# Reciprocal square roots of 35 row norms: a guess from ScalarE's Sqrt and one Newton step in place of an integer guess and three Newton steps

## The chip, the cores and the metric

The kernel is one program on one core of a Trainium2 chip. It runs one inference step of a small two-layer decoder trunk. The metric is device time in microseconds (us); the number compared is the median over runs. The profile comes from one profiled execution, whose own time stands beside its span below. The engines are named as in the profile: PE is the matrix engine, PEld its weight loads, DVE the vector engine, ACT the scalar engine, POOL the general engine, SP the engine that issues most of the DMAs ("SPq" in its rows). Each engine works through its instructions in order.

## The reference

The trunk has 1024 prompt rows and 64 sample rows of 1024 columns, and two layers. The first has an S5 mixer, the second attention over one shared K/V; each has a convolutional feed-forward block behind it. Around every block stands the same row norm. In the reference, cut to what matters here:

```python
def rmsnorm(x, g):
    xf = x.astype(jnp.float32)
    y = xf * lax.rsqrt(jnp.mean(xf * xf, axis=-1, keepdims=True) + NORM_EPS)
    return (y * g.astype(jnp.float32)).astype(x.dtype)
...
def trunk(x, ssm_h0, conv_buf0, past_k, past_v, p):
    for i in range(DEPTH):
        if i < N_A_LAYERS:
            ...
            x = x + rmsnorm(a_out, p['a_post_g'][i])
        else:
            ...
                kv_in = rmsnorm(x, p['kv_norm_g'])
                k_new = (kv_in @ p['w_k']).reshape(bsz, seq_len, N_HEADS, 2 * HEAD_DIM)
            ...
            x = x + rmsnorm(o @ p['w_o'][j], p['b_post_g'][j])
        f_out, buf = conv_ffn(rmsnorm(x, p['f_pre_g'][i]), conv_buf0[i], p['w_up'][i], p['conv_w'][i],
                              p['conv_b'][i], p['w_down'][i])
        x = x + rmsnorm(f_out, p['f_post_g'][i])
```

What matters is how `rsqrt` of one number per row is computed in the norms behind the output projection (`o @ p['w_o']`) and behind the two down projections (`f_out`), and in the norms of the next block that follow them at once.

## The kernel before

The rows lie in nine token tiles, eight of 128 rows and one of 64 (the samples). The stages follow one another: the S5 mixer and its GLU, the first feed-forward block (`ffn_up(0)`, `ffn_down(0)`), K/V and query projections (`kv_proj`), attention, the output projection (`o_proj`), the second feed-forward block (`ffn_up(1)`, `ffn_down(1)`). PE multiplies in a three-product form, each operand split into a high and a low part (`mm3`, L809 to L811, or L1417); `split_evac` makes such a pair, a CAST on ACT (L144) and a subtraction on DVE (L145).

A finished tile `y` of a projection passes through the "tail":

- `tail_a` closes the block: the sum of squares of the row (`square_sum`, a Square on ACT with an accumulator, L824), the product with the gain (DVE, L851), the reciprocal root `r` (`rstd_from`), then `y * r` plus the residual row in one instruction (DVE, L854). SP stores the result (L855); after the first down projection that is `x2d<-acc`, after the output projection `x3d<-acc`, after the second down projection the program's output.
- `tail_n` is the norm of the next block on that result: again `square_sum`, `rstd_from`, then the product with `r`, on ACT without a gain (L862) or on DVE with one (L864). After the second down projection there is none.
- `tail_b` (or `Combos.pair`) transposes the normed tile on PE (L870) and splits it into the operands `xT_hi` and `xT_lo` of the next projection.

`rstd_from` works on a column of 128 numbers. `rv` is -0.5 times the mean square plus epsilon (L120; L122 where a part of the sum was taken earlier). `rr` begins as an integer guess on the bits of `rv` (L123), and three Newton steps of two instructions follow (L130 writes `rs`, L134 writes `rr`). Each of these eight DVE instructions depends on the one before. With `aside` the Newton steps run on POOL instead.

`Tail` delays the steps: `tail_n` of a tile is issued right behind its `tail_a`, `tail_b` some tiles later. The instructions are not issued in program order: the program is built with a scheduler that simulates a timeline and sets each engine's order by it, so that a change of a few instructions moves others around them.

In `ffn_down`, the operand tiles of the next step are loaded by SP from the scratch tensor `gd` (`gr<-gd`, L1342 or L1355), cast by ACT and multiplied (L1417); partial sums are added to the `acc` tile of their token tile on DVE (L1424 in the last step of the first down projection, L1428 elsewhere). These loads, the residual rows `xr` (L847, L1383) and the stores of finished tiles share SP's queue, in order.

In `o_proj` the second half of the columns is done last, for the tiles in `LATE`; each is copied from PSUM by ACT (L2025), closed by `tail_a` and normed by `tail_n` with a gain (L864), while `ffn_up(1)` already prepares its weights: sums of weight tiles on DVE (L1109 to L1112) and their split into `whi` (ACT) and `wlo` (DVE).

Of the kernel before, what the change touches and what calls it, by code (L numbers as in the profile page):

```python
# [13 lines left out]
I32 = mybir.dt.int32  # L14
AF = mybir.ActivationFunctionType
ALU = mybir.AluOpType
# [5 lines left out]
D = 1024  # L22
# [23 lines left out]
RSQ_MAGIC = float(0x5F3759DF - (1 << 22) - (1 << 30))  # L46
# [27 lines left out]
def trunk_kernel(ctx, tc, I, O):  # L74
    nc = tc.nc
    V = nc.vector
    A = nc.scalar
# [4 lines left out]
    def nm(s):  # L82
        uid[0] += 1
        return f"{s}_{uid[0]}"
# [23 lines left out]
    def flat(t, n=512):  # L108
        return t[:, 0:n]

    def rstd_from(pool, ss, n, parts, tag, n_mean=D, bufs=None, pre=None, aside=False):


        kw = {"bufs": bufs} if bufs else {}
        v = pool.tile([P, n], F32, tag=tag + "v", name=nm("rv"), **kw)
        s = pool.tile([P, n], F32, tag=tag + "s", name=nm("rs"), **kw)
        r = pool.tile([P, n], F32, tag=tag + "r", name=nm("rr"), **kw)
        p = slice(0, parts)
        if pre is None:
            V.tensor_scalar(v[p], ss, -0.5 / n_mean, -0.5 * EPS, op0=ALU.mult, op1=ALU.add)  # L120
        else:
            V.scalar_tensor_tensor(v[p], ss, -0.5 / n_mean, pre, op0=ALU.mult, op1=ALU.add)  # L122
        V.tensor_scalar(r[p].bitcast(I32), v[p].bitcast(I32), -0.5, RSQ_MAGIC, op0=ALU.mult, op1=ALU.add)  # L123
        for _ in range(3):
            if aside:
                GP.tensor_scalar(s[p], r[p], r[p], v[p], op0=ALU.mult, op1=ALU.mult)
                GP.tensor_scalar(r[p], s[p], 1.5, r[p], op0=ALU.add, op1=ALU.mult)
                continue
            if n == 1:
                V.scalar_tensor_tensor(s[p], r[p], r[p], v[p], op0=ALU.mult, op1=ALU.mult)  # L130
            else:
                V.tensor_tensor(s[p], r[p], r[p], ALU.mult)
                V.tensor_tensor(s[p], s[p], v[p], ALU.mult)
            V.scalar_tensor_tensor(r[p], s[p], 1.5, r[p], op0=ALU.add, op1=ALU.mult)  # L134
        return r
# [616 lines left out]
    pools = {}  # L752
# [45 lines left out]
    def slot(tag, shape=None, dtype=F32):  # L798

        al = {"gx": "acc", "post": "acc", "junk": "gr"}  # L800
        shp, bufs = {"acc": ([P, 2 + SEQ + NB * 10], NACC), "gx": ([P, 4, 2 * P], NACC), "gr": ([P, 512], NGR),
                     "xr": ([P, D], 2), "junk": ([P, D], NGR), "post": ([P, D], NACC),
                     "cvo": ([P, 4, 18], 2), "cpar": ([P, 2 * NF, 20], 1), "ss": ([P, 1], 4)}[tag]
        tag = al.get(tag, tag)
        return pools["ph"].tile(shape or shp, dtype, tag=tag, name=nm(tag), bufs=bufs)
# [10 lines left out]
    def row_bcast(src):  # L816
        t = slot("post")
        nc.sync.dma_start(t, src.partition_broadcast(P))
        return t

    def square_sum(y, n):
        junk = slot("junk", dtype=BF16)
        ss = slot("ss")
        A.activation(junk[0:n, 0 : y.shape[1]], y, AF.Square, accum_out=ss[0:n])  # L824
        return ss[0:n]

    sums = {}
# [13 lines left out]
    def tail_a(y, tt, post, xsrc, xdst, last=False, rest=slice(0, D), aside=False, xr=None):  # L841


        t0, n = tokens(tt)
        if xr is None:
            xr = slot("xr")
            nc.sync.dma_start(xr[0:n], xsrc(tt))  # L847
        halves = (slice(512, D), slice(0, 512)) if last else (slice(0, D),)
        ss = square_sum(y[:, rest], n)
        for hs in halves if last else (rest,):  # L850
            V.tensor_tensor(y[:, hs], y[:, hs], post[0:n, hs], ALU.mult)  # L851
        r = rstd_from(pools["ph"], ss, 1, n, "n1", bufs=4, pre=sums.pop(tt, None), aside=aside)
        for hs in halves:
            V.scalar_tensor_tensor(y[:, hs], y[:, hs], r[0:n], xr[0:n, hs], op0=ALU.mult, op1=ALU.add)  # L854
            nc.sync.dma_start(xdst(tt)[:, hs], y[:, hs])  # L855

    def tail_n(y, tt, aside, gain=None):

        n = tokens(tt)[1]
        r = rstd_from(pools["ph"], square_sum(y, n), 1, n, "n1", bufs=4, aside=aside)  # L860
        if gain is None:
            A.mul(y, y, r[0:n])  # L862
        else:
            V.scalar_tensor_tensor(y, y, r[0:n], gain[0:n], op0=ALU.mult, op1=ALU.mult)  # L864
# [55 lines left out]
    class Tail:  # L920
# [2 lines left out]

        def __init__(self):
            self.n, self.q, self.combos, self.gain, self.lag = [], [], None, None, 2

        def add(self, y, tt, *a, aside=False, **kw):
            tail_a(y, tt, *a, aside=aside, **kw)
# [20 lines left out]
    tail = Tail()  # L949
# [422 lines left out]

    def ffn_down(dn, i, xsrc, xdst, norm):
        acc, res = {}, {}
        post = [None]
        nch = len(dn.plan)

# [619 lines left out]
    def o_proj():  # L1997

        ws = half_units(I["w_o"][0], 1)
        post = row_bcast(I["b_post_g"][0])  # L2000
        tail.gain, tail.lag = row_bcast(I["f_pre_g"][1]), 1
        conv_params(1)
        xsx = sample_pair()

        for half, tts in ((1, ORDER_O), (0, LATE)):
# [4 lines left out]
            for tt in tts:  # L2010
                if tt == 0 and half:
                    tail.combos = Combos()
                t0, n = tokens(tt)
                end = half == 0 or tt in EARLY
                if end:
                    y = slot("acc")[0:n, 0:D]
# [87 lines left out]
```

## Time and profile before

| | us |
|---|---|
| median of 3 runs | 2680.4 |
| lowest and highest run | 2679.09, 2680.55 |
| the profiled execution's own time | 2684.83 |
| its span | 2682.9 |
| DVE busy in the span | 1963.5 |
| ACT busy in the span | 1270.9 |
| DVE busy in all L130 (x156), L134 (x204), L123 (x88) | 30.3, 30.8, 13.0 |

A row of the profile's timeline gives the start in us from the span's start, the duration, the engine, the line, the operation, what it writes and reads, and in brackets the idle time before it and what ended that. A row of the windows gives for each engine its busy time in that stretch and the number of instructions, then the granted PE clock, the DMA share and GB/s. A row by line ends with the total and mean duration and the engine's idle time before such instructions. A row of the waits names the waiting instruction, what it waited for, the total, the times and the longest. A row of the chain gives start, length and piece. The durations of neighbouring rows overlap, as an engine starts an instruction before the one ahead of it has ended; how long one holds the engine is read from start to start.

### The profile page before, as it was taken

What the parts mean: (1) busy time and instruction counts of PE and PEld (TensorE: products, weight loads), DVE (VectorE), ACT (ScalarE), POOL (GpSimd) and SP (SyncE); (2) the same over time, 40 slices, a digit from 0 to 9 for tenths busy, and PEclk for the clock granted to TensorE, in tenths of its full rate; (3) what the DMA queues carried; (4) which work ended last, traced back from release to release, by engine and by line L of the source; (5) the groups of instructions that cost most, each with busy time, mean ns of one, the idle gap of its engine ahead of it and who ended that gap; (6) DMA issues with size and microseconds to landing.
All of it is one profiled execution on the core that took longest, in us unless ns stands there. A gap on an engine that the chain in (4) does not pass through costs nothing.

```text
span 2682.9 us, 39622 instructions
## 1 busy us (share of the span) xinstructions
PE 2500.6 (93%) x14234; PEld 2203.5 (82%) x14234; DVE 1963.5 (73%) x3683; ACT 1270.9 (47%) x2559; POOL 657.3 (24%) x1062
## 2 busy tenths in 40 slices
PE   3778998999999989999999899989799999998997
PEld 2777887999999967778777788877699999996775
DVE  7994358777777789984232688875877777778999
ACT  6763334444444454354322677764544444444432
POOL 3220030111111175501201222113011111137661
PEclk9999998999999999999999899999899999999998
DMA  5443233222222233444646433335322222233334
GB/s 145 99 98 88 85 124 124 65 83 74 74 74 74 89 116 92 127 145 166 204 157 211 104 79 95 97 105 171 115 69 79 74 74 74 74 104 107 94 102 145
DMA packets 265688, 286.77 MB, mean 107 GB/s; under 512 B 42268, under 2 KB 212564, under 8 KB 265492
## 3 DMA queue, kind: packets, MB, share of 16 engines
q1 hardware_dynamic: 261892, 273.55, 33.0%
q0 software_dynamic: 3088, 9.77, 1.7%
q8 instruction: 113, 1.85, 0.3%
q10 hardware_dynamic: 512, 0.92, 0.1%
q14 instruction: 83, 0.68, 0.1%
HBM read 193.58 MB, written 70.93 MB: 99 GB/s over the span
## 4 chain that ended last, share of the span: by engine, by line
PE 58%; DVE 13%; DMA 4%; issue 3%; ACT 3%; POOL 2%; SPq 0%; DVEq 0%; POOLq 0%; ACTq 0%
PE mm L809 17%; PE mm L810 17%; PE mm L811 17%; DVE acc L1428 2%; DMA gr<-gd 1%; DVE xT_lo L145 1%; DVE S L1898 1%; PE mm L1417 1%; ACT S L1902 1%; DVE wst L145 1%; DVE xT_hi L145 1%; DVE acc L854 1%; PE mm L1436 1%; PE tr L870 1%; PE mm L1926 1%
## 5 line engine op out<-in xcount | busy, mean ns | idle before, releaser
L809 PE MATMUL mm<-xT_hi,whi 128*128 128x384 f32 (+1 forms) x1408 | 457.0, 325 | 2.0 <-ACT acc L1146 1.8
L810 PE MATMUL mm<-xT_lo,whi 128*128 128x384 f32 (+1 forms) x1408 | 456.3, 324 | 1.6 <-DVE xT_lo L145 1.6
L811 PE MATMUL mm<-xT_hi,wlo 128*128 128x384 f32 (+1 forms) x1408 | 454.2, 324 | 0.0
L809 PEld LDWEIGHTS mm<-xT_hi,whi 128*128 128x128 f32 x1408 | 265.4, 189 | 3.8 <-ACT acc L1146 2.4
L810 PEld LDWEIGHTS mm<-xT_lo,whi 128*128 128x128 f32 x1408 | 265.7, 189 | 2.4 <-DVE xT_lo L145 2.3
L811 PEld LDWEIGHTS mm<-xT_hi,wlo 128*128 128x128 f32 x1408 | 265.4, 189 | 0.8
L1195 POOL COPY cvo<-acc 128x2 f32<-128x2 f32 x88 | 53.3, 606 | 818.5 <-ACT acc L1178 818.5
L809 PE MATMUL mm<-whi,xT_hi 128*128 128x512 f32 x608 | 243.9, 404 | 4.9 <-ACT whi L792 4.7
L1192 DVE SCALAR_TENSOR_TENSOR acc<-acc,cpar,acc 128x1104 f32<-128x1104 f32 x176 | 240.0, 1385 | 4.7 <-ACT acc L1190 4.6
L810 PE MATMUL mm<-wlo,xT_hi 128*128 128x512 f32 x608 | 241.9, 398 | 0.1
L811 PE MATMUL mm<-whi,xT_lo 128*128 128x512 f32 x608 | 241.7, 399 | 0.0
L144 ACT CAST whi<-raw 128x1024 fp32r<-128x1024 f32 x88 | 92.5, 1051 | 253.5 <-PE mm L811 245.2
L1428 DVE TENSOR_TENSOR acc<-mm,acc 128x512 f32<-128x512 f32 x279 | 184.7, 680 | 9.8 <-PE mm L811 9.3
L145 DVE TENSOR_TENSOR wlo<-raw,whi 128x1024 fp32r<-128x1024 f32 x88 | 107.7, 1224 | 107.0 <-PE mm L810 91.6
L809 PE MATMUL mm<-acc,whi 128*128 128x384 f32 x528 | 179.1, 339 | 0.0
L811 PE MATMUL mm<-acc,wlo 128*128 128x384 f32 x528 | 178.7, 339 | 0.0
L810 PE MATMUL mm<-acc,whi 128*128 128x384 f32 x528 | 178.3, 338 | 0.0
L809 PEld LDWEIGHTS mm<-whi,xT_hi 128*128 128x128 f32 x608 | 115.6, 191 | 36.2 <-ACT whi L792 5.6
L810 PEld LDWEIGHTS mm<-wlo,xT_hi 128*128 128x128 f32 x608 | 114.7, 189 | 27.8 <-DVE wlo L793 0.8
L811 PEld LDWEIGHTS mm<-whi,xT_lo 128*128 128x128 f32 x608 | 114.4, 188 | 27.6 <-issue 0.8
L1190 ACT ACTIVATE acc<-acc,cpar 128x1104 f32<-128x1104 f32 x88 | 114.1, 1311 | 18.1 <-DVE acc L1161 11.9
L145 DVE TENSOR_TENSOR wlo<-xr,whi 128x1024 fp32r<-128x1024 f32 x88 | 107.6, 1223 | 16.7 <-ACT whi L144 8.6
(572 smaller groups left out, 6255.9 us busy)
## 6 DMA issues: line engine op xcount, KB each, us to landing
raw<-in_w_up_dram SPq DMA_DIRECT2D x88, 512.0 KB
gd<-acc SPq DMA_DIRECT2D x44, 552.0 KB
raw<-in_w_down_dram SPq DMA_DIRECT2D x44, 512.0 KB
gr<-gd SPq DMA_DIRECT2D x80, 256.0 KB
raw<-in_glu_w_dram SPq DMA_DIRECT2D x40, 256.0 KB
acc<-in_cache_k_dram SPq DMA_DIRECT2D x16, 512.0 KB
acc<-in_cache_v_dram SPq DMA_DIRECT2D x16, 512.0 KB
xj<-in_x_prompt_dram SPq DMA_DIRECT2D x8, 512.0 KB
```

Of the source, the lines that this page charges most:

```text
L144: A.copy(hi_ap, ps_ap)
L145: V.tensor_tensor(lo_ap, ps_ap, hi_ap.bitcast(F32), ALU.subtract)
L809: PE.matmul(out, lh, rh, start=start, stop=False, **kw)
L810: PE.matmul(out, lh, rl, start=False, stop=False, **kw)
L811: PE.matmul(out, ll, rh, start=False, stop=stop, **kw)
L854: V.scalar_tensor_tensor(y[:, hs], y[:, hs], r[0:n], xr[0:n, hs], op0=ALU.mult, op1=ALU.add)
L870: PE.transpose(ps[:, c * n : (c + 1) * n], y[:, c * P : (c + 1) * P], ident[0:n, 0:n])
L1190: A.activation(hc, hb[:, 2 : 2 + TG], AF.Identity, bias=cp[:, ft, 3:4], scale=cp[:, ft, 2:3])
L1192: V.scalar_tensor_tensor(hc, hb[:, tap : tap + TG], cp[:, ft, tap : tap + 1], hc, op0=ALU.mult, op1=ALU.add)
L1195: GP.tensor_copy(co[:, 0:2], hb[:, SEQ : SEQ + 2])
L1417: PE.matmul(pa[h], lt, wt[:, h * 512 : (h + 1) * 512], start=st and j == 0, stop=sp and j == len(seq) - 1)
L1428: V.tensor_tensor(a, ps, a, ALU.add)
```

## The change

`rstd_from` gets an argument `root`. Where it is set and `aside` is not, the integer guess is replaced by a Sqrt on ACT of -2 times `rv` and a RECIPROCAL of it on DVE, and one Newton step follows in place of three. `Tail` gets a field `root`, false at first; `o_proj` and `ffn_down` set it, and `tail_a` and `tail_n` pass it on. `Tail.root` is not reset, so it holds from the first down projection on. Norms on POOL (`aside`) and the norms of the S5 stage and of attention remain as they were.

```diff
-    def rstd_from(pool, ss, n, parts, tag, n_mean=D, bufs=None, pre=None, aside=False):
+    def rstd_from(pool, ss, n, parts, tag, n_mean=D, bufs=None, pre=None, aside=False, root=False):
...
-        V.tensor_scalar(r[p].bitcast(I32), v[p].bitcast(I32), -0.5, RSQ_MAGIC, op0=ALU.mult, op1=ALU.add)
-        for _ in range(3):
+        root = root and not aside
+        if root:
+            A.activation(s[p], v[p], AF.Sqrt, scale=-2.0)
+            V.reciprocal(r[p], s[p])
+        else:
+            V.tensor_scalar(r[p].bitcast(I32), v[p].bitcast(I32), -0.5, RSQ_MAGIC, op0=ALU.mult, op1=ALU.add)
+        for _ in range(1 if root else 3):
...
-        r = rstd_from(pools["ph"], ss, 1, n, "n1", bufs=4, pre=sums.pop(tt, None), aside=aside)
+        r = rstd_from(pools["ph"], ss, 1, n, "n1", bufs=4, pre=sums.pop(tt, None), aside=aside, root=tail.root)
...
-        r = rstd_from(pools["ph"], square_sum(y, n), 1, n, "n1", bufs=4, aside=aside)
+        r = rstd_from(pools["ph"], square_sum(y, n), 1, n, "n1", bufs=4, aside=aside, root=tail.root)
...
             self.n, self.q, self.combos, self.gain, self.lag = [], [], None, None, 2
+            self.root = False
...
     def ffn_down(dn, i, xsrc, xdst, norm):
         acc, res = {}, {}
+        tail.root = True
...
-        tail.gain, tail.lag = row_bcast(I["f_pre_g"][1]), 1
+        tail.gain, tail.lag, tail.root = row_bcast(I["f_pre_g"][1]), 1, True
```

The lines behind the change carry other numbers: L851 becomes L857, L854 L860, L862 L868, L864 L870, L145 L151, L144 L150, L1424 L1433, L1428 L1437, L2025 L2034; the new Sqrt is L126, the RECIPROCAL L127, the Newton step L136 and L140. In the built program DVE has 140 instructions fewer, ACT has 35 Sqrts and three table loads more, and PE, POOL and SP have as many as before. Where the scheduler now puts things is shown at three places. In the names the first number is that of the tile and is the same in both programs.

First, DVE's queue near the end of the first down projection, before the change. acc_1323 and acc_1314 are two neighbouring output tiles, acc_1327 is the next one; L854 of acc_1314 lets SP store that tile and then issue the next load of gr:

```order
L851 TENSOR_TENSOR acc_1323_8851<-acc_1323_8851,acc_1539_10511 128x1024
...
L1424 TENSOR_TENSOR acc_1327_8878<-mm_1620_10876,acc_1327_8878 128x512
L1424 TENSOR_TENSOR acc_1327_8878<-mm_1621_10877,acc_1327_8878 128x512
...
L130 SCALAR_TENSOR_TENSOR rs_1592_10749<-rr_1593_10750,rv_1591_10748 128x1
L134 SCALAR_TENSOR_TENSOR rr_1598_10766<-rs_1597_10765,rr_1598_10766 128x1
L134 SCALAR_TENSOR_TENSOR rr_1610_10831<-rs_1609_10830,rr_1610_10831 128x1
L134 SCALAR_TENSOR_TENSOR rr_1593_10750<-rs_1592_10749,rr_1593_10750 128x1
L130 SCALAR_TENSOR_TENSOR rs_1597_10765<-rr_1598_10766,rv_1596_10764 128x1
L130 SCALAR_TENSOR_TENSOR rs_1609_10830<-rr_1610_10831,rv_1608_10829 128x1
L854 SCALAR_TENSOR_TENSOR acc_1314_8818<-acc_1314_8818,rr_1593_10750,xr_1588_10742 128x1024
```

And with the change:

```order
L136 SCALAR_TENSOR_TENSOR rs_1592_10734<-rr_1593_10735,rv_1591_10733 128x1
L140 SCALAR_TENSOR_TENSOR rr_1593_10735<-rs_1592_10734,rr_1593_10735 128x1
L857 TENSOR_TENSOR acc_1323_8851<-acc_1323_8851,acc_1539_10511 128x1024
L860 SCALAR_TENSOR_TENSOR acc_1314_8818<-acc_1314_8818,rr_1593_10735,xr_1588_10727 128x1024
L121 TENSOR_SCALAR rv_1608_10808<-ss_1607_10805 128x1
...
L136 SCALAR_TENSOR_TENSOR rs_1597_10747<-rr_1598_10748,rv_1596_10746 128x1
L1433 TENSOR_TENSOR acc_1327_8878<-mm_1620_10849,acc_1327_8878 128x512
L1433 TENSOR_TENSOR acc_1327_8878<-mm_1621_10850,acc_1327_8878 128x512
...
L136 SCALAR_TENSOR_TENSOR rs_1609_10809<-rr_1610_10810,rv_1608_10808 128x1
L140 SCALAR_TENSOR_TENSOR rr_1610_10810<-rs_1609_10809,rr_1610_10810 128x1
L860 SCALAR_TENSOR_TENSOR acc_1323_8851<-acc_1323_8851,rr_1610_10810,xr_1605_10802 128x1024
```

The residual addition of acc_1314 stood behind the two L1424 of acc_1327, which wait for PE; it now stands ahead of them, directly behind the gain product of acc_1323. On ACT, in the same place, before the change (acc_1308 is the tile that PE transposes next, acc_1619 the operand that the load of gr_1618 brings):

```order
L824 ACTIVATE gr_1611_10842,ss_1612_10843<-acc_1314_8818 128x1024
L862 ACTIVATE acc_1308_8790<-acc_1308_8790,rr_1598_10766 128x1024
L824 ACTIVATE gr_1623_10906,ss_1624_10907<-acc_1327_8878 128x1024
L824 ACTIVATE gr_1628_10923,ss_1629_10924<-acc_1323_8851 128x1024
L144 CAST xT_hi_75<-tr_1633_10938 128x4x128
L824 ACTIVATE gr_1640_10987,ss_1641_10988<-acc_1331_8903 128x1024
L144 CAST acc_1619_10872<-gr_1618_10871 128x4x128
```

And with the change:

```order
L830 ACTIVATE gr_1611_10818,ss_1612_10819<-acc_1314_8818 128x1024
L126 ACTIVATE rs_1609_10809<-rv_1608_10808 128x1
L830 ACTIVATE gr_1623_10879,ss_1624_10880<-acc_1327_8878 128x1024
L126 ACTIVATE rs_1614_10822<-rv_1613_10821 128x1
L150 CAST acc_1619_10845<-gr_1618_10844 128x4x128
L868 ACTIVATE acc_1308_8790<-acc_1308_8790,rr_1598_10748 128x1024
L830 ACTIVATE gr_1628_10893,ss_1629_10894<-acc_1323_8851 128x1024
```

The product L862 (now L868) of acc_1308 stood ahead of the cast of gr_1618 and now stands behind it; two Sqrts stand ahead of that cast.

Second, DVE's queue at the end of the output projection, before the change. acc_3416 and acc_3431 are the last two tiles that are normed for `ffn_up(1)`, wlo_3489 is the low part of a weight tile that has to be loaded first:

```order
L145 TENSOR_TENSOR wlo_3489_19052<-raw_3484_19041,whi_3488_19051 128x1024
L134 SCALAR_TENSOR_TENSOR rr_3443_18743<-rs_3442_18742,rr_3443_18743 128x1
L1109 TENSOR_TENSOR xr_3486_19045<-raw_3485_19043 128x512
L145 TENSOR_TENSOR acc_3268_17917<-tr_3451_18784,acc_3264_17913 128x2x128
L130 SCALAR_TENSOR_TENSOR rs_3456_18806<-rr_3457_18807,rv_3455_18805 128x1
L1111 TENSOR_TENSOR xr_3487_19046<-raw_3484_19041,raw_3485_19043 128x512
L145 TENSOR_TENSOR acc_3268_17917<-tr_3452_18793,acc_3264_17913 128x128
L864 SCALAR_TENSOR_TENSOR acc_3416_18615<-acc_3416_18615,rr_3443_18743,acc_3235_17778 128x1024
L1110 TENSOR_TENSOR xr_3486_19045<-xr_3486_19045,raw_3484_19041 128x512
...
L864 SCALAR_TENSOR_TENSOR acc_3431_18691<-acc_3431_18691,rr_3457_18807,acc_3235_17778 128x1024
```

And with the change:

```order
L870 SCALAR_TENSOR_TENSOR acc_3416_18552<-acc_3416_18552,rr_3443_18671,acc_3235_17724 128x1024
...
L151 TENSOR_TENSOR wlo_3467_18758<-xr_3461_18744,whi_3466_18757 128x1024
L127 RECIPROCAL rr_3457_18732<-rs_3456_18731 128x1
...
L151 TENSOR_TENSOR wlo_3489_18974<-raw_3484_18963,whi_3488_18973 128x1024
L1117 TENSOR_TENSOR xr_3486_18967<-raw_3485_18965 128x512
L1119 TENSOR_TENSOR xr_3487_18968<-raw_3484_18963,raw_3485_18965 128x512
L140 SCALAR_TENSOR_TENSOR rr_3457_18732<-rs_3456_18731,rr_3457_18732 128x1
L151 TENSOR_TENSOR acc_3269_17864<-tr_3452_18718,acc_3265_17860 128x3x128
L1160 TENSOR_TENSOR acc_3470_18765<-mm_3473_18772,acc_3471_18768 128x384
...
L1118 TENSOR_TENSOR xr_3486_18967<-xr_3486_18967,raw_3484_18963 128x512
L151 TENSOR_TENSOR xT_lo_76<-tr_3476_18807,xT_hi_75 128x4x128
L870 SCALAR_TENSOR_TENSOR acc_3431_18622<-acc_3431_18622,rr_3457_18732,acc_3235_17724 128x1024
```

The norm product of acc_3416 stood behind wlo_3489 and now stands ahead of it; that of acc_3431 still stands behind it, with eight rows between. ACT's queue shortly before, where the first of these tiles is copied from PSUM, as it was:

```order
L824 ACTIVATE gr_3398_18536,ss_3399_18537<-acc_3395_18506 128x512
L144 CAST acc_3262_17911<-tr_3370_18387 128x3x128
L824 ACTIVATE gr_3406_18583,ss_3407_18584<-acc_3403_18553 128x512
L144 CAST acc_3263_17912<-tr_3371_18396 128x2x128
L2025 COPY acc_3416_18615<-mm_3417_18617 128x512
L144 CAST acc_3263_17912<-tr_3370_18387 128x128
L144 CAST acc_3264_17913<-tr_3371_18396 128x2x128
L144 CAST whi_3468_18839<-raw_3459_18819 128x1024
L144 CAST acc_3264_17913<-tr_3372_18405 128x128
```

And with the change:

```order
L830 ACTIVATE gr_3398_18482,ss_3399_18483<-acc_3395_18452 128x512
...
L830 ACTIVATE gr_3406_18526,ss_3407_18527<-acc_3403_18496 128x512
L150 CAST acc_3263_17858<-tr_3371_18342 128x2x128
L126 ACT_TABLE_LOAD
L126 ACTIVATE rs_3401_18487<-rv_3400_18486 128x1
L2034 COPY acc_3416_18552<-mm_3417_18554 128x512
L150 CAST acc_3263_17858<-tr_3370_18333 128x128
L126 ACTIVATE rs_3409_18531<-rv_3408_18530 128x1
L150 CAST acc_3264_17859<-tr_3371_18342 128x2x128
L150 CAST whi_3468_18761<-raw_3459_18741 128x1024
```

The table load and the first Sqrt now stand ahead of the copy of acc_3416, the second Sqrt ahead of the cast of whi_3468.

Third, the end of DVE's queue, before the change (acc_4006, acc_4013 and acc_4023 are the last three output tiles):

```order
L134 SCALAR_TENSOR_TENSOR rr_4299_25560<-rs_4298_25559,rr_4299_25560 128x1
L134 SCALAR_TENSOR_TENSOR rr_4309_25595<-rs_4308_25594,rr_4309_25595 128x1
L134 SCALAR_TENSOR_TENSOR rr_4304_25577<-rs_4303_25576,rr_4304_25577 128x1
L854 SCALAR_TENSOR_TENSOR acc_4006_23441<-acc_4006_23441,rr_4299_25560,raw_4265_25330 128x1024
L130 SCALAR_TENSOR_TENSOR rs_4308_25594<-rr_4309_25595,rv_4307_25593 128x1
L130 SCALAR_TENSOR_TENSOR rs_4303_25576<-rr_4304_25577,rv_4302_25575 128x1
L134 SCALAR_TENSOR_TENSOR rr_4309_25595<-rs_4308_25594,rr_4309_25595 128x1
L134 SCALAR_TENSOR_TENSOR rr_4304_25577<-rs_4303_25576,rr_4304_25577 128x1
L130 SCALAR_TENSOR_TENSOR rs_4308_25594<-rr_4309_25595,rv_4307_25593 128x1
L854 SCALAR_TENSOR_TENSOR acc_4013_23490<-acc_4013_23490,rr_4304_25577,xr_4279_25428 128x1024
L134 SCALAR_TENSOR_TENSOR rr_4309_25595<-rs_4308_25594,rr_4309_25595 128x1
L854 SCALAR_TENSOR_TENSOR acc_4023_23536<-acc_4023_23536,rr_4309_25595,raw_4285_25447 128x512 x2
```

And with the change:

```order
L136 SCALAR_TENSOR_TENSOR rs_4298_25463<-rr_4299_25464,rv_4297_25462 128x1
L136 SCALAR_TENSOR_TENSOR rs_4303_25477<-rr_4304_25478,rv_4302_25476 128x1
L140 SCALAR_TENSOR_TENSOR rr_4299_25464<-rs_4298_25463,rr_4299_25464 128x1
L140 SCALAR_TENSOR_TENSOR rr_4304_25478<-rs_4303_25477,rr_4304_25478 128x1
L860 SCALAR_TENSOR_TENSOR acc_4006_23363<-acc_4006_23363,rr_4299_25464,raw_4265_25243 128x1024
L860 SCALAR_TENSOR_TENSOR acc_4013_23412<-acc_4013_23412,rr_4304_25478,xr_4279_25338 128x1024
L857 TENSOR_TENSOR acc_4023_23458<-acc_4023_23458,acc_4217_24999 128x512 x2
L121 TENSOR_SCALAR rv_4307_25491<-ss_4306_25487 128x1
L127 RECIPROCAL rr_4309_25493<-rs_4308_25492 128x1
L136 SCALAR_TENSOR_TENSOR rs_4308_25492<-rr_4309_25493,rv_4307_25491 128x1
L140 SCALAR_TENSOR_TENSOR rr_4309_25493<-rs_4308_25492,rr_4309_25493 128x1
L860 SCALAR_TENSOR_TENSOR acc_4023_23458<-acc_4023_23458,rr_4309_25493,raw_4285_25354 128x512 x2
```

The Newton rows of three tiles were interleaved with one another up to the last product; now the last tile's five instructions stand by themselves at the end, with the RECIPROCAL waiting for the Sqrt on ACT.

## The prediction

> **What bounds the kernel now.** I read the page's shares first, then windows of 10 us around the stages whose code changes, then the rows inside them.
>
> ```profile
> PE 2500.6 (93%) x14234; PEld 2203.5 (82%) x14234; DVE 1963.5 (73%) x3683; ACT 1270.9 (47%) x2559; POOL 657.3 (24%) x1062
> core 0: us, PE busy (x) PEld busy (x) DVE busy (x) ACT busy (x) POOL busy (x), PEclk, DMA share, GB/s
> 1180.00:1190.00 10.00, 7.83 (x38) 6.08 (x36) 9.70 (x33) 4.75 (x10) 0.00 (x0) 1.00 0.38 104
> 1190.00:1200.00 10.00, 7.74 (x21) 5.69 (x22) 9.34 (x39) 7.24 (x12) 0.00 (x0) 0.66 0.46 172
> 1900.00:1910.00 10.00, 2.87 (x10) 2.28 (x11) 10.00 (x40) 4.25 (x9) 0.24 (x2) 0.56 0.58 209
> 2660.00:2670.00 10.00, 6.75 (x24) 4.78 (x22) 9.96 (x32) 2.49 (x5) 0.00 (x0) 0.89 0.33 117
> ```
>
> PE is busy 93% of the span, so a shorter VectorE (DVE) chain is worth nothing in most of it. It can be worth something only where PE has holes while DVE is full, and these windows are such places: D, the end of the first down projection (1180 to 1200); O, the last tiles of the output projection (from 1900); K, the kernel's end (from 2640). All three are stages with changed norms. What is saved elsewhere counts as nothing, since PE covers it.
>
> **What the change removes.** The built program has 140 fewer rows on DVE, four for each of 35 norms: 18 in the first down projection, 8 in O, 9 in the second down projection. Per norm one L123, two L130 and two L134 go, a RECIPROCAL comes, and ScalarE (ACT) gets a Sqrt. A run of such rows near the end, with start and duration:
>
> ```profile
> 2673.60 0.16 DVE L134 SCALAR_TENSOR_TENSOR rr<-rs,rr 128x1 f32<-128x1 f32 x1
> 2673.67 0.16 DVE L123 TENSOR_SCALAR rr<-rv 128x1 int32<-128x1 int32 x1
> 2673.73 0.16 DVE L134 SCALAR_TENSOR_TENSOR rr<-rs,rr 128x1 f32<-128x1 f32 x1
> 2673.80 0.48 DVE L130 SCALAR_TENSOR_TENSOR rs<-rr,rv 128x1 f32<-128x1 f32 x3
> 2674.19 0.30 DVE L134 SCALAR_TENSOR_TENSOR rr<-rs,rr 128x1 f32<-128x1 f32 x3
> ```
>
> From start to start an L123 or L134 holds DVE for 0.07 us and an L130 for 0.13 (three in 0.39). Removed: 0.07 + 2 x 0.13 + 2 x 0.07 = 0.47 us. The added RECIPROCAL has a row elsewhere, in the groups by line:
>
> ```profile
> L1648 DVE RECIPROCAL ssl<-ssl 128x1 f32<-128x1 f32 x8 | 1.3, 164 | 5.0 <-ACT acc L1647 4.9
> ```
>
> It lasts as long as an L134 (164 ns), so I book it at 0.07: net 0.40 us per norm, 14 us of DVE in all, of which only what stands on a chain counts. A 128x1 Sqrt isn't in this trace. The nearest row is ACT's one-column read of an accumulator:
>
> ```profile
> L824 ACT ACTIVATION_READ_ACCUMULATOR gr<-acc 128x1 f32 (+1 forms) x83 | 15.6, 188 | 0.0
> ```
>
> At 188 ns I take 0.2 us, and up to 0.6 with a hand-over of a DVE row's length on either side. With the Sqrts come three table loads, one per stage; a load that is already there, and what follows it:
>
> ```profile
> 484.87 1.28 ACT L1198 ACT_TABLE_LOAD   x1
> 486.17 1.13 ACT L1198 ACTIVATE acc<-acc 128x1104 f32<-128x1104 f32 x1
> ```
>
> It holds ACT for 1.28 us, and the next instruction starts right behind. In D the load falls near 1155, ahead of this row:
>
> ```profile
> 1158.58 1.06 ACT L824 ACTIVATE gr<-acc 128x1024 bf16<-128x1024 f32 x1 [3.80 <-DVE rr L134]
> ```
>
> ACT idles 3.80 us there, so it costs nothing; without that gap it would be 1.28. In O and K it can cost 0 to 1.28 each. (The Trainium skill, "ScalarE: Activation LUTs", section "What ACT_TABLE_LOAD costs", adds about 1380 ns of drain to the 1283 ns, 2.66 us for a switch, and so speaks against three more of them: by it the worst loss in O and in K would be 1.4 us larger. The row agrees on the 1283 ns and shows no such gap behind it.)
>
> **D: a load queued behind a norm.** PE's timeline:
>
> ```profile
> 1187.54 1.10 PE L870 MATMUL tr<-ident,acc 128*128 128x128 f32 x8 [0.80 <-ACT acc L862]
> 1191.65 1.22 PE L1417 MATMUL mm<-whi,acc 128*128 128x512 f32 x2 [3.01 <-ACT acc L144]
> ```
>
> PE idles 0.80 + 3.01 = 3.81 us, the second time for the cast of a gr tile. SP issues that tile's load right behind the store of a finished tile:
>
> ```profile
> 1185.23 0.32 SPq L855 DMA_DIRECT2D x2d<-acc  x1
> 1185.64 0.39 SPq L1342 DMA_DIRECT2D gr<-gd  x1
> ```
>
> and the store waits for L854 on DVE:
>
> ```profile
> 1179.13 1.23 DVE L851 TENSOR_TENSOR acc<-acc,acc 128x1024 f32<-128x1024 f32 x1
> ...
> 1183.91 1.29 DVE L854 SCALAR_TENSOR_TENSOR acc<-acc,rr,xr 128x1024 f32<-128x1024 f32 x1
> ```
>
> Between this L851 and L854 stand two L1424, which need PE's results, and twelve rows of guess and Newton. In the changed order the L854 of that tile stands directly behind this L851, so at about 1180.3 (1179.13 + the 1.15 that such a row holds DVE): end 1181.6, load issued near 1182.0, 3.6 us earlier. How long the load takes, from the one before it (its issue on SP, the cast that waited for it) and from the chain of waits:
>
> ```profile
> 1174.84 0.37 SPq L1342 DMA_DIRECT2D gr<-gd  x1
> ```
>
> ```profile
> 1178.79 0.62 ACT L144 CAST acc<-gr 128x512 fp32r<-128x512 f32 x1 [0.63 <-DMA gr<-gd]
> ```
>
> ```profile
> 1187.55 6.09 DMA gr<-gd
> ...
> 1194.33 10.15 PE mm L1417 x36
> ...
> 1205.80 1.82 PE mm L1417 x8
> ```
>
> One took 3.9 us to its cast (1174.84 to 1178.79), one 6.09. With 3.9 the cast starts at 1185.9, before PE is free (1187.54 - 0.80 = 1186.74): no wait. With 6.09 it ends at 1188.6, a wait of 1.9. I take 3.9, as stores and loads are further apart now than at 1185 to 1188. The L862 that PE waited 0.80 for is newly queued behind this cast on ACT and ends at 1187.6; but four matmuls now stand ahead of its transposes on PE (4 x 0.23 = 0.9, to 1187.65), so that wait goes too. The next load follows near 1186, lands by 1192.2 even at 6.09, and is wanted behind 8 transposes and 20 matmuls, near 1193.3.
>
> After the wait the clock is 0.66: 36 matmuls take 10.15 us, where the rate of 1205.80 (8 in 1.82) gives 8.19, 1.96 less; and the four matmuls from 1191.65 to 1194.33 take 2.68 in place of 0.91, 1.77 less. Of these 3.7 I take 2.2, the second part and a little, since a rest of idle time may keep some slow matmuls. (The Trainium skill, "TensorE: Matmul & The Clock Gate", Part 1, has the array at half clock after about 3.4 us of idling; here it is slow after 3.01, so the trace sets the threshold lower. By the page's rule, with no wait left, all 3.7 would go and D be 1.5 us better.) **D: -6.0**, bounds -7.5 (all of it) and +1 (the wait stays, because a RECIPROCAL that waits for its Sqrt holds L854 where it was).
>
> **O: DVE is late for PE's transposes.** From the table of waits, PE's timeline and DVE's:
>
> ```profile
> PE tr L870 <- DVE acc L864: 11.7, 2, 6.8
> ```
>
> ```profile
> 1933.17 1.07 PE L870 MATMUL tr<-ident,acc 128*128 128x128 f32 x8
> ```
>
> ```profile
> 1923.88 1.23 DVE L145 TENSOR_TENSOR wlo<-raw,whi 128x1024 fp32r<-128x1024 f32 x1 [2.72 <-ACT whi L144]
> ...
> 1926.95 1.28 DVE L864 SCALAR_TENSOR_TENSOR acc<-acc,rr,acc 128x1024 f32<-128x1024 f32 x1
> ...
> 1929.28 0.56 DVE L145 TENSOR_TENSOR acc<-tr,acc 128x384 fp32r<-128x384 f32 x1
> 1929.75 0.69 DVE L1112 TENSOR_TENSOR xr<-raw,xr 128x512 f32<-128x512 f32 x1
> 1930.35 0.22 DVE L130 SCALAR_TENSOR_TENSOR rs<-rr,rv 128x1 f32<-128x1 f32 x1
> ```
>
> PE waits twice, 6.8 and 4.9 us. The first wait stays: the Newton rows saved ahead of the first L864 (two norms and part of a third, 0.9 us) are taken back by the table load and the Sqrts' place on ACT. The second is for the L864 at 1926.95, which stands behind a wlo that waits 2.72 us for a weight load; in the changed order that tile's row stands ahead of the wlo. But then the next tile is late: its row stands behind this wlo and eight rows, five of 512 columns (0.60 each, as from 1929.75 to 1930.35), two of 384 (0.47, from 1929.28 to 1929.75) and one Newton row: 4.0 us. The wlo hangs on a transfer and comes no earlier, so 1923.88 + 1.14 + 4.0 = 1929.0, and done at 1930.3. PE waits there, but goes on at 1930.3 and not at 1933.17, 2.8 us; I keep 2.5, since ACT's cast ahead of the wlo now has Sqrts in its queue. **O: -2.5**, bounds -5 (the wait of 4.9 goes whole) and +1 (most of ACT's load of 1.28 lands on the chain, nothing else moves).
>
> **K: DVE is full to the end.** With 9.96 of 10 us busy, DVE's own time counts: 9 norms x 0.40 = 3.6 us. Against it the last tile has nothing left to hide its chain behind (0.15 + 0.2 + 0.16 + 0.22 + 0.16 for rv, Sqrt, RECIPROCAL and the Newton step, 0.9 us), and the table load may cost half of its 1.28. **K: -2.0**, bounds -4 (3.6 and a shorter wait of PE) and +1.5 (load and chain uncovered, DVE's saving lost in waits).
>
> Sum: -6.0 - 2.5 - 2.0 = -10.5 us. The profiled execution took 2684.83 (span 2682.9), so it would be 2674.3; against the median of 2680.4 it is **2669.9**.
>
> **Rivals.** First, that little reaches PE: **within 0.2%** (5.4 us, about what a measurement of this kernel can tell). ACT and DVE work in order, and a RECIPROCAL now stands in DVE's queue for a Sqrt, which stands behind a square that waits for DVE's result of another tile. Where this round trip is late, every L1424 and L854 behind it is late. For it: D's Sqrt does stand behind such a square. Against it: ACT is idle for more than half of D's first window (4.75 of 10 us busy). It would leave D with a wait of 1.9 and the slow matmuls (-1.9), O and K at -0.5 each: -2.9, 2677.5.
>
> Second, **slower**: Sqrts hold up ACT's copies and casts in O. ACT's timeline before:
>
> ```profile
> 1893.48 0.60 ACT L2025 COPY acc<-mm 128x512 f32<-128x512 f32 x1
> ...
> 1897.78 1.06 ACT L824 ACTIVATE gr<-acc 128x1024 bf16<-128x1024 f32 x1 [1.00 <-DVE acc L854]
> ```
>
> The copy of 1893.48, without idle time ahead of it, would stand behind the table load and a Sqrt; a second Sqrt stands ahead of the whi cast. The load of 1.28, and for each Sqrt up to 1.3 us, the time of a 1024-wide row on DVE behind which its rv may be stuck, make 3.9 for O's first wait; the load and one such wait make 2.6 in K; with D unchanged, +6.5, 2686.9. It decides from where the delay passes ACT's idle time, of which the 1.00 us ahead of 1897.78 is the first large piece. Against it: ACT is busy only 4.25 of 10 us from 1900 on. Third, that the change does other than it says and the tables alternate (a load back for each square or cast, 70 x 1.28 = 90 us): the built program has three more loads, not 70, so below one in a hundred.
>
> **How the numbers follow.** Forecast 0.64 (a gain over 0.2%, smaller sums included), first rival 0.26, slower 0.10. The range joins the forecast with the first rival: the low end has all three at their lower bounds, -16.5; the high end D and O at their upper ones and K at nothing, +2: 2664 to 2682.
>
> **What would show it.** Right: no wait of 3 us at an L144 cast near 1187, the clock at 1.00 from 1190 to 1200, the first down projection's last matmul 6 us earlier; in O two waits at transposes still, the second ending near 1930; at the end DVE still full. Wrong: DVE idle ahead of RECIPROCALs, gr<-gd transfers slower than 6 us, casts late behind Sqrts, or a stage after D or O that gives the gain back by waiting for weights.

## The result and the profile after

The changed kernel runs in 2664.98 us (median; 2660.08 to 2665.99) against 2680.41 us before: ratio 0.9937, with a 95% interval of 0.9922 to 0.9952. A second comparison on another chip (e11 below) gave 2664.12 against 2680.07, ratio 0.9942 (0.9929 to 0.9955). So it is faster by about 15.4 us, where the forecast sum was 10.5; the time lies at the low edge of the range.

The program has the same 14,234 matmuls before and after, so the start of the n-th one can be compared between two profiles, and the three stages can be cut at the same matmuls: D from the 6106th to the 6400th, O from the 9656th to the 10400th, K from the 14050th to the end of the span. Against the profiled execution before, that of the changed kernel (2665.99 us) is shorter by 7.3 us in D, 4.1 in O and 4.8 in K, 16.2 together; 2.6 more lie in stages that no edit touched. Such parts vary from one execution to the next by several us in every kernel here, so below the stages are compared, not only the whole.

The windows of the changed kernel that answer to those of before (O and K have moved forward by some 11 and 15 us):

```profile
core 0: us, PE busy (x) PEld busy (x) DVE busy (x) ACT busy (x) POOL busy (x), PEclk, DMA share, GB/s
1180.00:1190.00 10.00, 10.00 (x50) 8.36 (x49) 9.93 (x27) 7.69 (x17) 0.00 (x0) 1.00 0.82 263
1190.00:1200.00 10.00, 10.00 (x50) 8.36 (x49) 10.00 (x23) 7.77 (x14) 0.00 (x0) 1.00 0.37 115
1890.00:1900.00 10.00, 4.04 (x14) 3.45 (x15) 9.97 (x27) 5.10 (x15) 1.21 (x2) 0.66 0.65 219
2645.00:2655.00 10.00, 5.28 (x18) 3.38 (x17) 10.00 (x25) 2.93 (x7) 0.00 (x0) 0.79 0.60 218
```

In D PE is now busy all the time, at full clock, while DVE is as full as before. In O and K PE still has its holes and DVE is still full.

**D after.** The residual addition, SP's store and the load behind it, ACT's cast, and PE's transposes, from the timelines of the changed kernel:

```profile
1177.28 1.23 DVE L857 TENSOR_TENSOR acc<-acc,acc 128x1024 f32<-128x1024 f32 x1 [0.17 <-ACT gr L830]
1178.42 1.28 DVE L860 SCALAR_TENSOR_TENSOR acc<-acc,rr,xr 128x1024 f32<-128x1024 f32 x1
```

```profile
1179.73 0.32 SPq L861 DMA_DIRECT2D x2d<-acc  x1
1180.14 0.39 SPq L1350 DMA_DIRECT2D gr<-gd  x1
```

```profile
1184.30 0.62 ACT L150 CAST acc<-gr 128x512 fp32r<-128x512 f32 x1
1184.83 1.15 ACT L868 ACTIVATE acc<-acc,rr 128x1024 f32<-128x1024 f32 x1
```

```profile
1186.77 1.03 PE L876 MATMUL tr<-ident,acc 128*128 128x128 f32 x8
1187.56 1.17 PE L1426 MATMUL mm<-whi,acc 128*128 128x512 f32 x4
```

The load is issued at 1180.14 in place of 1185.64, and the cast is done before PE asks for it. PE's rows have no bracket: it doesn't wait, and four matmuls take 1.17 us and no longer 2.68 (of which 0.61 was a wait, see below).

**O after.** PE's waits, and ACT ahead of the first of them:

```profile
1894.84 1.94 PE L876 MATMUL tr<-ident,acc 128*128 128x128 f32 x8 [5.85 <-DVE acc L870]
...
1915.67 0.41 PE L815 MATMUL mm<-acc,whi 128*128 128x384 f32 x1 [2.53 <-DVE acc L1160]
...
1918.66 1.93 PE L876 MATMUL tr<-ident,acc 128*128 128x128 f32 x8
```

```profile
1883.60 1.28 ACT L126 ACT_TABLE_LOAD   x1
1884.90 0.20 ACT L126 ACTIVATE rs<-rv 128x1 f32<-128x1 f32 x1
1885.01 0.57 ACT L2034 COPY acc<-mm 128x512 f32<-128x512 f32 x1
```

The first wait is 5.85 us where it was 6.82. The second is 2.53, and no longer for the norm of acc_3416 but for an accumulation on DVE. The table load and the Sqrt do stand ahead of the copy, and cost it 1.4 us; a Sqrt takes 0.20.

**K after.** The last tile's chain on DVE:

```profile
2658.67 0.15 DVE L121 TENSOR_SCALAR rv<-ss 128x1 f32<-128x1 f32 x1
2659.09 0.16 DVE L127 RECIPROCAL rr<-rs 128x1 f32<-128x1 f32 x1 [0.27 <-ACT rs L126]
2659.29 0.22 DVE L136 SCALAR_TENSOR_TENSOR rs<-rr,rv 128x1 f32<-128x1 f32 x1
2659.54 0.16 DVE L140 SCALAR_TENSOR_TENSOR rr<-rs,rr 128x1 f32<-128x1 f32 x1
2659.74 1.42 DVE L860 SCALAR_TENSOR_TENSOR acc<-acc,rr,raw 128x512 f32<-128x512 f32 x2
```

From rv to the addition it is 1.07 us, with 0.27 of idle time for the Sqrt. The stage is 4.8 us shorter all the same.

### The profile page after: what moved, and what is told of

The parts are those of the page before. It is cut to its first block, busy times and chain, and to the rows that moved or that the text cites. A ratio compares the mean times of both kernels' runs of the same rounds, so it can differ in the third digit from the quotient of the medians.

```text
span 2664.1 us, 39516 instructions
## 1 busy us (share of the span) xinstructions
PE 2493.7 (94%) x14234; PEld 2199.5 (83%) x14234; DVE 1947.8 (73%) x3543; ACT 1281.0 (48%) x2597; POOL 661.2 (25%) x1062
## 4 chain that ended last, share of the span: by engine, by line
PE 58%; DVE 13%; DMA 4%; issue 4%; ACT 3%; POOL 3%; SPq 0%; DVEq 0%; ACTq 0%; POOLq 0%
PE mm L815 17%; PE mm L817 17%; PE mm L816 17%; DVE acc L1437 2%; PE mm L1426 2%; DVE xT_lo L151 2%; DMA gr<-gd 2%; DVE S L1907 1%; ACT S L1911 1%; DVE xT_hi L151 1%; DVE wst L151 1%; PE mm L1935 1%; PE tr L876 1%; DVE acc L860 1%; POOL xr L1306 1%
## 5 line engine op out<-in xcount | busy, mean ns | idle before, releaser
L150 ACT CAST whi<-raw 128x1024 fp32r<-128x1024 f32 x88 | 92.7, 1053 | 248.5 <-PE mm L817 245.1
L1437 DVE TENSOR_TENSOR acc<-mm,acc 128x512 f32<-128x512 f32 x279 | 184.3, 679 | 8.4 <-PE mm L817 8.1
L151 DVE TENSOR_TENSOR wlo<-raw,whi 128x1024 fp32r<-128x1024 f32 x88 | 107.7, 1224 | 103.5 <-PE mm L816 90.8
L1186 ACT COPY acc<-mm 128x256 f32<-128x256 f32 x88 | 32.4, 369 | 183.7 <-PE mm L817 183.7
```

The source lines that it names most:

```text
L150: A.copy(hi_ap, ps_ap)
L151: V.tensor_tensor(lo_ap, ps_ap, hi_ap.bitcast(F32), ALU.subtract)
L1186: A.copy(hb[:, 2 + n0 : 2 + SEQ], ps[:, 0:wp])
L1437: V.tensor_tensor(a, ps, a, ALU.add)
```

## The experiments

Each was timed beside the kernel before on its own chip, and profiled once. The table gives the stages of the profiled execution against the profiled one before; a dash marks a stage that the kernel leaves as it was, with the difference that it shows anyway in parentheses: this is how far a stage varies by itself.

| kernel | median, before beside it (us) | ratio (95%) | D | O | K |
|---|---|---|---|---|---|
| changed kernel | 2664.98, 2680.41 | 0.9937 (0.9922 to 0.9952) | -7.3 | -4.1 | -4.8 |
| e11, the same again | 2664.12, 2680.07 | 0.9942 (0.9929 to 0.9955) | -7.3 | -3.7 | -4.3 |
| e1, first down projection alone | 2672.48, 2679.58 | 0.9975 (0.9965 to 0.9986) | -7.3 | - (-0.5) | - (+0.3) |
| e2, output projection alone | 2676.00, 2679.58 | 0.9990 (0.9981 to 1.0000) | - (+0.4) | -4.4 | - (+0.2) |
| e3, second down projection alone | 2673.51, 2679.58 | 0.9982 (0.9971 to 0.9992) | - (+0.1) | - (-1.9) | -5.7 |
| e4, integer guess, one step | 2661.00, 2679.58 | 0.9940 (0.9923 to 0.9956) | -7.2 | -7.0 | -5.0 |
| e5, integer guess, two steps | 2673.44, 2681.28 | 0.9967 (0.9954 to 0.9980) | -2.7 | +0.1 | -3.3 |
| e6, Sqrt guess, three steps | 2686.43, 2681.28 | 1.0020 (1.0009 to 1.0031) | -3.3 | -1.4 | +1.3 |
| e7, stores of x2d on POOL | 2687.72, 2681.28 | 1.0024 (1.0016 to 1.0033) | +5.6 | - (+0.4) | - (+0.6) |
| e8, table load taken early | 2662.77, 2681.28 | 0.9928 (0.9915 to 0.9941) | -7.3 | -6.1 | -5.1 |
| e9, before, loads asked for earlier | 2672.46, 2680.07 | 0.9969 (0.9957 to 0.9981) | -6.4 | - (-2.0) | - (+0.8) |
| e10, two spare steps per norm | 2674.76, 2680.07 | 0.9976 (0.9966 to 0.9987) | -1.6 | -1.7 | -3.5 |

### One stage at a time

```diff
 e1, ffn_down:  -tail.root = True    +tail.root = norm       (and False in o_proj)
 e2, ffn_down:  -tail.root = True    +tail.root = False
 e3, ffn_down:  -tail.root = True    +tail.root = not norm   (and False in o_proj)
```

> Sqrt guess and one Newton step in the first down projection alone; the output projection and the second down projection as before. Theory (the three stages add, each through its own queue): the wait of PE at the gr cast near 1191 is gone and the time falls by the 7.7 us that lie in this stage between the two profiled programs, to about 2672.7. Rival (the gain of this stage is given back later, in attention or in the output projection): less than 3 us, above 2677.4.

> Sqrt guess and one Newton step in the output projection alone. Theory (stages add): -4.2 us as between the profiled programs, to about 2676.2, with one wait of PE for L870 near 6 us and none of 4.8. Rival (only the second wait counts, as I had it): -2.7, 2677.7. Rival (the gain came in with what the first down projection saved): 0, 2680.4.

> Sqrt guess and one Newton step in the second down projection alone. Theory (DVE is full there, and its rows count one for one): 3.7 us of rows, and 0.9 us less between DVE's last row and the end, -4.9 us, to about 2675.5. Rival (my sum: the last chain and the table load take 1.6 back): -2.0, 2678.4.

By medians they gave -7.1, -3.6 and -6.1 us, 16.8 together; the whole change gave 15.4 and 16.0. Within the noise the stages add, each came out near its theory, and none gives its gain back. The rivals for D and K fall: 3 us at most, or 2.0. For O, 2.7 can't be told from 3.6 by these times; its profile says -4.4, where O alone moves by up to 2 us in kernels that don't touch it.

### What ACT's part costs

> As the changed kernel in all 35 norms, but the guess is the integer one on DVE, with one Newton step: two Newton steps are left out, no Sqrt and no table load is there, and DVE has as many rows as in the changed kernel. Theory (the gain is DVE's rows alone, ACT's part is hidden): the same as the changed kernel within 1.5 us, 2663.5 to 2666.5. Rival (Sqrts and table loads cost on the path, up to 1.28 us each in the output projection and at the end): 2 to 4 us below the changed kernel, 2661 to 2663.

```diff
-        if root:
-            A.activation(s[p], v[p], AF.Sqrt, scale=-2.0)
-            V.reciprocal(r[p], s[p])
-        else:
+        if True:
             V.tensor_scalar(r[p].bitcast(I32), v[p].bitcast(I32), -0.5, RSQ_MAGIC, op0=ALU.mult, op1=ALU.add)
```

Without ACT's part O is 2.9 us shorter than in the changed kernel, and D and K are the same. The median, 2661.0, is the rival's, though by the ratios e4 and the changed kernel can't be told apart. PE's first wait in O, in e4:

```profile
1886.94 1.94 PE L873 MATMUL tr<-ident,acc 128*128 128x128 f32 x8 [4.41 <-DVE rr L137]
```

It is 4.41 against 5.85, and the second fell from 2.53 to 1.25. In K and D the table loads were hidden.

> The changed kernel with one more Sqrt at the start of the output projection, so that the table load falls there and no longer ahead of the first norm of its last tiles. Theory (the table load of 1.28 us is most of what ACT's part costs in the output projection): PE's first wait there falls from 5.85 to about 4.6 us and the time by 1.3 us against the changed kernel, to about 2663.7. Rival (the hand-overs from DVE to ACT and back are the cost, or the load is hidden): no change, 2665.

```diff
         xsx = sample_pair()
+        warm = slot("ss")
+        A.activation(warm, tail.gain[:, 0:1], AF.Sqrt)
```

The load moved to where PE has other work, and the first wait answers (ACT, then PE, in e8):

```profile
1805.51 1.28 ACT L2014 ACT_TABLE_LOAD   x1
```

```profile
1895.14 1.94 PE L876 MATMUL tr<-ident,acc 128*128 128x128 f32 x8 [4.64 <-DVE acc L870]
```

4.64 for 5.85 is 1.2 us, the length of the load, as the theory has it; of the 1.4 us that separate the changed kernel from e4 at this wait that is nearly all. So e8 is a version with the changed kernel's arithmetic and a shorter first wait in O. Its ratio, 0.9928, lies below those of the changed kernel, but the intervals overlap, so the times alone don't show it to be faster.

### D: is it the load behind the store?

> The kernel before with its three Newton steps, but the stores of the first down projection's finished tiles are issued by POOL, so that SP's loads of gr no longer stand behind a store that waits for DVE. Theory (the load behind the store is what PE waited for): the wait of 3.0 us at the cast near 1191 and the slow matmuls behind it go, -4 to -7, 2673 to 2676, with no norm changed. Rival (the load waits for something else, its buffer or the transfer itself, or PE then waits for the normed tile, whose Newton rows are as late as before): 0 to -2, 2678 to 2680.

```diff
-            nc.sync.dma_start(xdst(tt)[:, hs], y[:, hs])
+            (GP if tail.pool else nc.sync).dma_start(xdst(tt)[:, hs], y[:, hs])
```

(`tail.pool` is set in the first down projection alone.) Both theories missed: it was slower, with a longer wait at the same cast and another at the next one. SP's queue, a transfer and PE's two waits, in e7:

```profile
1183.63 0.33 SPq L847 DMA_DIRECT2D xr<-x1d  x1
1184.07 0.38 SPq L1343 DMA_DIRECT2D gr<-gd  x1
1185.48 0.33 SPq L847 DMA_DIRECT2D xr<-x1d  x1
1185.90 0.45 SPq L1343 DMA_DIRECT2D gr<-gd  x1
```

```profile
1185.90 7.67 DMA gr<-gd
```

```profile
1190.47 1.22 PE L1419 MATMUL mm<-whi,acc 128*128 128x512 f32 x2 [5.67 <-ACT acc L144]
...
1194.26 1.22 PE L1419 MATMUL mm<-whi,acc 128*128 128x512 f32 x2 [1.72 <-ACT acc L144]
```

The store is gone from SP's queue, but the load of gr that PE waits 5.67 us for (1184.07) now stands behind the load of a residual row xr (1183.63), which starts when an L854 ends (1182.32 to 1183.6 in e7), since xr has two buffers and L854 reads from them. So the load is tied to the same instruction as before. It takes 5.7 us to its cast (1189.80), and the next load, of 1185.90, takes 7.67, with POOL's stores under way beside them. The kernel did not take away what it was meant to. e9 does, by asking for each tile's load one tile earlier:

> The kernel before with its three Newton steps and DVE's order unchanged, but in the first down projection's last step the loads of gr are asked for one tile earlier, so that the load PE waited for stands behind the store of the tile before (acc_1308) and no longer behind that of acc_1314. Theory (the load behind the late store is what PE waited for): no wait of 3 us at a cast near 1191, no slow matmuls behind it, first down projection -5 to -7.5, 2673 to 2676. Rival (PE then waits as long for the normed tile or for DVE to free its accumulators, because DVE's Newton rows are as late as before): 0 to -2, 2678 to 2681.

```diff
             if kind == "p":
-                dn.upto(k + 2)
+                dn.upto(k + (3 if c else 2))
```

SP's queue, and the windows of e9:

```profile
1173.69 0.32 SPq L855 DMA_DIRECT2D x2d<-acc  x1
1174.11 0.39 SPq L1342 DMA_DIRECT2D gr<-gd  x1
1174.58 0.79 SPq L847 DMA_DIRECT2D xr<-x1d  x1
1184.51 0.32 SPq L855 DMA_DIRECT2D x2d<-acc  x1
1184.92 0.39 SPq L1342 DMA_DIRECT2D gr<-gd  x1
```

```profile
1180.00:1190.00 10.00, 10.00 (x46) 8.28 (x45) 9.71 (x32) 5.32 (x9) 0.00 (x0) 1.00 0.47 131
1190.00:1200.00 10.00, 10.00 (x50) 8.34 (x49) 10.00 (x32) 3.79 (x6) 0.00 (x0) 1.00 0.38 146
```

The store at 1184.51 is nearly as late as before (1185.23). All Newton steps are still there, and up to this store DVE's order differs from that of before in a few rows only (two subtractions of operands and two Newton rows), so it is not quite unchanged. The load PE needed is the one of 1174.11 (its cast starts at 1177.48), PE doesn't wait, and the clock stays at 1.00: 6.4 us of D's 7.3, without touching a norm. The rival falls.

What e9 doesn't separate is the load from the place of its cast on ACT. In the profile before, the cast that PE waited 3.01 us for has no idle time ahead of it:

```profile
1189.94 1.06 ACT L824 ACTIVATE gr<-acc 128x1024 bf16<-128x1024 f32 x1
...
1190.99 0.61 ACT L144 CAST acc<-gr 128x512 fp32r<-128x512 f32 x1
```

The load of 1185.64 had landed at 1190.0, by its semaphore, so the last 1.0 us of that wait was ACT's queue. In e9 as in the changed kernel the earlier load also has its cast ahead of those rows of ACT.

### Rows or chain?

> Integer guess with two Newton steps in the 35 norms: one Newton step is left out, no Sqrt. Per norm DVE saves 0.20 us, and not 0.40. In DVE's order the residual addition of acc_1314 stands ahead of the two rows that wait for PE, and the norm of acc_3416 ahead of wlo_3489, as in the changed kernel. Theory (in the first down projection and for the second wait of the output projection the place in the order decides, at the end the number of rows): first down projection -7, output projection -4 or more (no Sqrt there), end about -2 to -3, so -13 to -15, 2665 to 2667. Rival (the gain goes with the number of rows everywhere): half of that of one step, about -9, 2671.

```diff
-        for _ in range(1 if root else 3):
+        for _ in range(2 if root else 3):
```

(with the integer guess of e4). It gave 7.8 us, clear of the theory's 13 to 15; the rival's 9 lies within the interval, but the stages don't follow it (half of the changed kernel's would be -3.6, -2.0 and -2.4): D -2.7, O nothing, K -3.3. The place in the order, which it shares with the changed kernel, is not enough. PE waits in D once more for a cast, one tile earlier:

```profile
1179.52 0.74 PE L1423 MATMUL mm<-whi,acc 128*128 128x512 f32 x2 [1.63 <-ACT acc L147]
```

> Sqrt guess, but all three Newton steps: DVE has the RECIPROCAL in place of the integer guess and otherwise the rows of before, and ACT has the Sqrts and table loads. Theory (the gain is DVE's rows and what their number does to the order; ACT's part is a cost, 2.9 us in the output projection by the run with the integer guess): no gain in the first down projection or at the end, 0 to 3 us slower in the output projection, 2680 to 2684. Rival (a better guess path on ACT is itself a gain): below 2676.

```diff
-        for _ in range(1 if root else 3):
+        for _ in range(3):
```

It is slower by 5 us, as the theory had the sign, but not where it had it: D gained 3.3, and of the loss most lies in the second feed-forward block between O and K, where the scheduler's other order makes PE wait in places it didn't before. So this run says that a Sqrt without fewer Newton steps is no gain, and little on the single stages.

> The changed kernel with two more Newton steps per norm computed on spare columns that nobody reads: DVE has 3669 rows, as before the change, but the chain to each residual addition is the short one. Theory (at the end DVE is full and its rows count): of the gain at the end (4.8 us) 3.6 are lost; in the first down projection and in the output projection some of the gain stays, since the additions may stand ahead of the spare rows; altogether 2670 to 2676. Rival (the length of the chain decides, not DVE's time): the changed kernel's time, 2665.

```diff
+        if root:
+            s2 = pool.tile([P, n], F32, tag=tag + "s2", name=nm("s2"), **kw)
+            r2 = pool.tile([P, n], F32, tag=tag + "r2", name=nm("r2"), **kw)
+            for a in (r, r2):
+                V.scalar_tensor_tensor(s2[p], a[p], a[p], v[p], op0=ALU.mult, op1=ALU.mult)
+                V.scalar_tensor_tensor(r2[p], s2[p], 1.5, a[p], op0=ALU.add, op1=ALU.mult)
```

Altogether 5.3 us are left of the gain, within the theory's range, but the stages split against it. DVE has 3683 rows in this trace, as in that of before. In D the rows count: of 7.3 us only 1.6 are left, with PE waiting 3.3 us for a subtraction on DVE:

```profile
1192.57 0.63 PE L882 MATMUL tr<-ident,acc 128*128 128x128 f32 x4 [3.33 <-DVE xT_lo L157]
```

In K they cost less than their own time: the spare rows hold DVE for 3.3 us, and 1.3 of the 4.8 us are lost. Up to the last spare row DVE idles 0.07 us in this stage, where it idles 1.40 in the changed kernel up to its last addition, so about 1.3 us of spare rows stand where DVE would have waited; another 0.5 us of them fall behind the last addition. So in K this run doesn't decide between the number of rows and the length of the chain.

### The changed kernel again

> The changed kernel itself, beside the kernel before on this chip, so that the three places can be read in a second profile. All theories: 2663 to 2667; first down projection -7.3, output projection -4 to -4.5, end -4.8 to -5.5.

It was run unedited beside e9 and e10. Ratio and stages came out as the first time, O with 3.7 for 4.1 us, so the stage differences of the changed kernel hold to some tenths of a us.

## Why the sum was too small

**Where the kernel is bound** was right. The three stages carry the gain, one by one and together, and PE covers the rest.

**D, -6.0 forecast, -7.3 measured: right in mechanism, one term too small.** The residual addition went directly behind the gain product and the load was issued 5.5 us earlier (forecast 3.6). It took 4.2 us from its issue to the cast, near the 3.9 taken and not the 6.09 feared; L868 behind the cast was in time. e9 shows that asking for the load earlier, with its cast, carries most of it. The step that failed is "Of these 3.7 I take 2.2": all of the slow matmuls went, since no idle time was left. Nor was all of the 3.7 slow matmuls: the second part, 1.77, holds a third wait of PE, for the next cast:

```profile
1194.33 1.22 PE L1417 MATMUL mm<-whi,acc 128*128 128x512 f32 x2 [0.61 <-ACT acc L144]
```

So the 7.3 us are 4.4 of idle time (0.80, 3.01 and 0.61), where 3.8 were forecast, and 2.9 of slow matmuls, where 2.2 were. Here the trace agrees with the Trainium skill, "TensorE: Matmul & The Clock Gate", Part 1, in that without the gap there is no slow stretch (1.00 in both windows). Of the 1.5 us more that its rule gave for D, 1.3 came.

**O, -2.5 forecast, -3.7 to -4.4 measured: the part behind the first wait right in size, the first wait wrong.** From the end of the first wait to the end of the stage the changed kernel gains 2.7 us, against 2.8 worked out and 2.5 kept, but not by the forecast wait: PE reached the last tile's transposes at 1918.66, just behind its norm, and had waited 2.53 us for an accumulation before. So that agreement is in part luck. "The first wait stays" failed: it fell by 1.0 us, in spite of the table load (e2 and e11 show 5.83 and 5.84). e4 and e8 show that the load was on the path, 1.2 us of it, as the slower rival had it for this place; DVE's shorter rows were worth more than that. Kernels that leave O as it was differ there by up to 2 us, so more can't be said of this term's size.

**K, -2.0 forecast, -4.3 to -5.7 measured, beyond its bound of -4: this is the largest miss.** The failed step is "Against it the last tile has nothing left to hide its chain behind (...), and the table load may cost half of its 1.28". The sum took 1.6 us back for these two. Only 0.4 was taken back: DVE's idle time, from the stage's start to its last addition, rose from 0.98 us to 1.40 (0.27 of it for the last Sqrt; it is 1.63 in e11 and 0.37 in e3), and the load fell at 2615, where PE was busy throughout. Most of the stage, before and then in the changed kernel:

```profile
2620.60:2667.60 47.00, 43.43 (x177) 33.71 (x175) 46.06 (x111) 16.52 (x34) 9.85 (x16) 0.96 0.37 118
```

```profile
2606.66:2652.50 45.84, 42.22 (x177) 33.08 (x175) 44.82 (x88) 19.34 (x42) 9.77 (x16) 0.98 0.46 149
```

The rows saved are as forecast: Newton rows hold DVE for 3.1 us in place of 6.9, 3.8 for the 3.6 of the sum. DVE's other rows took 0.5 us less in this profile, and 0.1 less in e11's. What the sum didn't have at all is the stretch behind DVE's last addition, which is 0.9 us shorter. The ends of both programs, up to DVE's last row (before, then the changed kernel):

```profile
2670.00:2679.00 9.00, 0.00 (x0) 0.00 (x0) 8.96 (x27) 0.96 (x2) 0.00 (x0) 0.64 1.01 357
2679.00:2682.90 3.90, 0.00 (x0) 0.00 (x0) 0.00 (x0) 0.00 (x0) 0.00 (x0) 0.50 0.57 224
```

```profile
2652.00:2661.10 9.10, 0.86 (x3) 0.14 (x1) 8.72 (x20) 1.56 (x4) 0.00 (x0) 0.50 0.70 285
2661.10:2664.10 3.00, 0.00 (x0) 0.00 (x0) 0.06 (x1) 0.00 (x0) 0.00 (x0) 0.50 0.45 175
```

Before, the finished tiles' stores kept the DMA engines full (1.01) to DVE's end, and 3.9 us followed; with the change the additions come earlier, the share is 0.70, and 3.0 us follow. In all six profiles with one Newton step in the second down projection this stretch is 2.98 to 3.01 us, in the seven others 3.9 to 4.5. That it is due to a backlog of stores is read from these rows; no run tested it alone.

**The rivals.** That little reaches PE didn't happen: in D the Sqrt behind a square was in time. The slower one had its mechanism in O (1.2 us of table load, 2.9 us by the profile of e4 for all of ACT's part) and not its size. The third is out: three loads, not 70.

## What to carry to other kernels

When a serial chain of tiny instructions sits ahead of a store and loads queue behind that store, look first at the queue: asking for the load one tile earlier was worth nearly as much (6.4 of 7.3 us) as shortening the chain. In a stage where one engine is full to the end, check what an uncovered last link costs before booking it (here 0.4 us, where 1.6 was booked), and count the stretch behind that engine's last row, which became 0.9 us shorter here. A function of another table set should have its table loaded where its engine is idle, not at its first use on the path: one spare Sqrt did that here.

## What the runs showed that was not expected

In D a load of gr took from 3.4 us (e9, 1174.11 to its cast at 1177.48) to 7.67 (e7, with POOL's stores beside it). Spare Newton rows took back 5.7 of 7.3 us in D, where PE came to wait for DVE, and 1.3 of 4.8 in K, where 1.3 us of them filled DVE's idle time. And executions of one kernel varied by up to 15 us on one chip (2669.59 to 2684.59 in 29 runs of the kernel before), so differences of 2 us were read from the stages' own rows and not from the totals.
